# RWKV in a hybrid decoder step: the norm of the key as a scale of tokens in the chunk inverse instead of a factor of the features

## The chip, the core and the metric

The kernel runs on one core of one Trainium2 chip. The metric is the device time of one execution in microseconds (us), as the median of several runs. Time before the change: 991.74 us (three runs, 990.62 to 992.3).

## What is computed

One step of a layer in which two branches run beside each other on the same normalised input: a linear-attention branch (RWKV-7, 8 heads of 64 features) and a differential attention. Gates merge them, and a squared-ReLU MLP follows. There are 512 prompt tokens and 8 sequences of 8 tokens, 576 in all. The change lies in the RWKV branch. Cut to that:

```python
kk = hs((k * lp['k_k']).astype(f32))
kk = kk / jnp.maximum(jnp.linalg.norm(kk, axis=-1, keepdims=True), 1e-12)
k = k.astype(f32) * (1.0 + (a - 1.0) * lp['k_a'].astype(f32))
S, y = rwkv7_scan(S0, hs(r), hs(decay), hs(k), hs(v), -kk, kk * hs(a))
# scan, for each token:
sa = jnp.einsum('bhij,bhj->bhi', S, a_t)          # a_t = -kk
S = S * w_t + sa[..., None] * b_t + v_t[..., None] * k_t   # b_t = kk * a
y_t = jnp.einsum('bhij,bhj->bhi', S, r_t)
```

Each key is divided by its norm over the 64 features of its head. The normalised key enters the recurrence twice, as `-kk` and as `kk * a`, so that the square of the inverse norm stands in the product of the two.

## The kernel before, in words

Everything that is dense is streamed through TensorE (PE): a weight block of 128 columns comes in by DMA, ScalarE (ACT) makes a rounded half of it (`hi_...`), VectorE (DVE) the rest (`lo_...`), and three products for each slice of 128 features (high by high, high by low, low by high, lines 190 to 196, each over 288 tokens) accumulate in PSUM. In the trace and in the order these products are named after what they write: `ps_z` are the RWKV projections (function `shifted`, line 424), `ps_g` the gates (`gate`, line 444), `ps_brb` the attention branch's output projection (`branch_b`), and later `ps_bra`, `ps_wo`, `ps_dn` and the MLP's. All of them are issued by PE in a fixed order.

The RWKV branch works on four pairs of heads (`rwkv(hp)`, line 742), with tokens in chunks of 64: eight of the prompt and a ninth that holds the 64 sample tokens. For a pair the stages are:

1. Preparation. `sq` is the square of the scaled key (line 753), five small products `pn` sum it over the features of a head (line 756), `nr` is the sum with a floor, raised to -0.5 on GpSimd (POOL, line 760). POOL then spreads each token's factor over 64 columns (`nb`, line 763). Four transposes `pk` and one `pks` on PE (lines 791 to 793) turn that into feature layout in PSUM, and two DVE instructions (lines 794 and 796) multiply it with the key and `k_k` to `kk`, which overwrites `sq`. Meanwhile the products `pw` and `pa` (lines 769 and 772), ACT and DVE make the decays (`u`, `cum`, `pe`, `pinv`, `pm`), `aa`, `k2` and `rkp`; `pbn` (line 807) is a product of `rkp`. `KB` and `ST` (lines 814 to 821) are the scaled keys and receptances; `pA` (line 833) is their product for every chunk, which DVE masks into `ABR` and `ST`.
2. `pV`, `pK` are transposes, `pI` (line 865) the product with the sample tokens' states.
3. The inverse (lines 878 to 927): a unit triangular matrix of every chunk is inverted in blocks of 32 tokens by doubling. `DT` is a copy of the diagonal blocks, `Y` and its 32x32 transpose `X` the first level. Each of four levels has 32x32 products `pW`, an ACT copy `W`, products `pZ`, the DVE addition `X<-X,pZ` and the transpose `Y<-X`. `pWc` and `pC` then make the block off the diagonal, and ACT puts the parts together in `TT`. Between `pW`, `pZ`, `pWc` and `pC` the call `take(9)` (line 894) puts nine streamed products, so that PE has work while ACT and DVE answer.
4. `chain(pr)` (line 994): the eight chunks one after the other for two pairs together (`pch` in four roles; DVE and ACT between them).
5. The output of a pair (lines 946 to 983): group norm, transposes `pTy`, products `pg` with the output gate, and the vector `oa`.

How many streamed products stand between those stages is written by hand: `waiting` is a list of streams that have yet to run, and `take(n)` (line 216) issues the next n products of it at that place. Lines 1084 to 1104 hold the order of the stages and these numbers. A list scheduler then fixes the order of each engine's instructions, and `fill` keeps some products behind a given one. When the list is empty, `take` issues nothing; it is filled again behind the last inverse (line 1097).

Of the kernel before, what the change touches and what calls it, by code (L numbers as in the profile page):

```python
# [8 lines left out]
F32 = mybir.dt.float32  # L9
# [3 lines left out]
ALU = mybir.AluOpType  # L13
AX = mybir.AxisListType

P = 128
D = 1024
KT = D // P
NPR = 512
# [7 lines left out]
NCH = 9  # L27
# [5 lines left out]
V_MU, V_W0, V_A0, V_KK, V_KA, V_RK, V_LW, V_LB, V_GM, V_GF, V_GO, V_SUB, V_END = (  # L33
    0, 14, 18, 22, 26, 30, 34, 38, 42, 50, 58, 66, 67)
# [7 lines left out]
def tile_hybrid_step(ctx, tc, xT, xsT, ktab, vtab, s0T, ptab, w_in, vecs, w2a2, g2, lamv,  # L42
# [3 lines left out]
    PE, VE, AE, GE = nc.tensor, nc.vector, nc.scalar, nc.gpsimd  # L46
    PS = bass.MemoryType.PSUM

    def pool(name, bufs=1, stack=ctx, **kw):
        return stack.enter_context(tc.tile_pool(name=name, bufs=bufs, **kw))  # L50
# [6 lines left out]
    def act(out, in_, func=AF.Copy, **kw):  # L57
        ring["act"] = AE.activation(out=out, in_=in_, func=func, **kw)  # L58

    def tt(out, a, b, op, eng=None):  # L60
        ins = (eng or VE).tensor_tensor(out=out, in0=a, in1=b, op=op)  # L61
        if eng is None:
            ring["tt"] = ins

    def stt(out, a, s, b, op0, op1):
        VE.scalar_tensor_tensor(out=out, in0=a, scalar=s, in1=b, op0=op0, op1=op1)

    def ts(out, a, s1, op0, s2=None, op1=ALU.bypass, eng=None):
        (eng or VE).tensor_scalar(out=out, in0=a, scalar1=s1, scalar2=s2, op0=op0, op1=op1)

    def mm(out, lhsT, rhs, start=True, stop=True):
        ring["mm"] = PE.matmul(out=out, lhsT=lhsT, rhs=rhs, start=start, stop=stop)  # L72
        return ring["mm"]

    def tr(out, in_, idn):
        ring["mm"] = PE.transpose(out=out, in_=in_, identity=idn)
# [14 lines left out]
    MUL, ADD, SUB, MAX = ALU.mult, ALU.add, ALU.subtract, ALU.max  # L91
# [7 lines left out]
    stat = pool("stat", 2)  # L99

    def bank(name):
        return psw.tile([P, 512], F32, tag="w", name=name)

    def tbank(name):
        return psc.tile([P, 512], F32, tag="t", name=name)

    def cbank(i, name):
        return (psy if i else psc).tile([P, 512], F32, tag=f"c{i}", name=name)
# [3 lines left out]
    c = const.tile([P, C_END], F32, name="cst_sb")  # L112
    nc.scalar.dma_start(out=c, in_=cst)
    ident = c[:, C_ID:C_ID + P]
# [8 lines left out]
    mhalf = const.tile([P, 20], F32, name="mhalf")  # L123
# [10 lines left out]
    def v(i, n=1):  # L134
        return vec[:, i:i + n]
# [80 lines left out]
    def take(n):  # L216

        while waiting and n:
            if next(waiting[0], None) is None:
                waiting.pop(0)  # L220
            else:
                n -= 1
# [38 lines left out]
    rc = pool("rc", stack=ph1)  # L261
# [9 lines left out]
    with tc.tile_pool(name="xin", bufs=2, reuse_waits="tile") as xin:  # L271
# [6 lines left out]
        for k in range(0, KT, 4):  # L278
            for j in range(3):
                with prio(FEED + 1000 + 10 * k + j):  # L280
                    name = f"raw_{'qkv'[j]}0_{k}"
                    if k == 0:
                        raw = ring["pool"].tile([P, 4, P], F32, tag="raw", name=name, bufs=3)
                    else:
                        raw = zw.tile([P, 1 + NX], F32, tag="z" if j else "tz", name=name,
                                      bufs=2 if j else 1)[:, :4 * P].rearrange("p (k w) -> p k w", k=4)
# [12 lines left out]
        for k in range(KT):  # L299
            if k == 0:  # L300
                act(acc, xt[k], AF.Square)
            else:
                sq = xin.tile([P, NT], F32, name="sq")
# [10 lines left out]
    ts(mu1, v(V_MU, 14), -1.0, MUL, 1.0, ADD, GE)  # L314
    hw0 = rc.tile([P, 8], F32, name="hw0")
    ts(hw0, v(V_W0, 8), 0.5, MUL, 0.0, ADD, GE)
    ka2 = rc.tile([P, 8], F32, name="ka2")
    ts(ka2[:, 0:4], v(V_KA, 4), 0.5, MUL, 0.0, ADD, GE)
    ts(ka2[:, 4:8], v(V_KA, 4), -0.5, MUL, 1.0, ADD, GE)
# [345 lines left out]
    for h in range(HB):  # L665
        if h:
            qkv(h)
        for cc in range(2):
            GE.tensor_copy(
                out=qbd[64 * cc:64 * cc + 64, :, h, 8 * cc:8 * cc + 8],  # L670
                in_=qT[64 * cc:64 * cc + 64, h, NPR:].rearrange("p (b q) -> p b q", b=NB))
# [45 lines left out]
    rt = pool("rt", 2, stack=rk, reuse_waits="tile")  # L717

    def ch(a):
        return a.rearrange("p (c t) -> p c t", t=64)  # L720

    def m3(ap_, n):
        q, w = ap_.shape
        return ap_.rearrange("p (o w) -> p o w", o=1).broadcast_to([q, n, w])
# [15 lines left out]
    halves = [(par, slice(64 * par, 64 * par + 64)) for par in range(2)]  # L740

    def rwkv(hp):
        e = hp % 2
        own = pair.setdefault(hp // 2, {})
        hs = slice(hp * P, (hp + 1) * P)
        r, k, vv = Pt[hp], Pt[4 + hp], Pt[8 + hp]

        def tmp(tag, bufs=1):
            return rt.tile([P, NT], F32, tag="T", name=f"{tag}_{hp}", bufs=6)


        sq = tmp("sq")
        act(sq, k, AF.Square, scale=v(V_KK + hp))
        pn = bank(f"pn{hp}")
        for t, o in enumerate(toks):
            mm(pn[:, 2 * t:2 * t + 2], sq[:, o:o + P], c[:, C_HS:C_HS + 2])
        (fill if hp != 2 else take)(8)
        nr = stat.tile([P, 10], F32, tag="nr", name=f"nr{hp}")
        ts(nr, pn[:, 0:10], 1e-24, MAX)
        GE.tensor_tensor(out=nr, in0=nr, in1=mhalf[:, :10], op=ALU.pow)  # L760

        nb = rt.tile([P, 5, P], F32, tag="G", name=f"nb{hp}", bufs=3)
        own["nb"] = GE.tensor_copy(out=nb.rearrange("p t (a d) -> p (t a) d", a=2),
                       in_=nr.rearrange("p (a o) -> p a o", o=1).broadcast_to([P, 10, 64]))
        u = tmp("u")
        aa = tmp("aa")
        for t0, n in HALF:
# [15 lines left out]
        pinv = tmp("pinv")  # L783
        act(pinv, cum, AF.Exp, scale=KAPPA)
        tt(cum, cum, u, SUB)
        pm = u
        act(pm, cum, AF.Exp, scale=-KAPPA)

        kk = sq
        pk, pks = bank(f"pk{hp}"), bank(f"pks{hp}")  # L790
        for t in range(4):
            tr(pk[:, t * P:(t + 1) * P], nb[:, t], ident)
        tr(pks[:, :P], nb[:, 4], ident)
        stt(kk[:, :NPR], k[:, :NPR], v(V_KK + hp), pk, MUL, MUL)
        pk = pks
        stt(kk[:, NPR:], k[:, NPR:], v(V_KK + hp), pk[:, 64:P], MUL, MUL)


        k2 = tmp("k2")
        act(k2, aa, AF.Identity, scale=ka2[:, hp:hp + 1], bias=ka2[:, 4 + hp:5 + hp])  # L800
        tt(k2, k2, k, MUL)
# [7 lines left out]


        KB = rt.tile([P, NCH, 2, 64], F32, tag="KB", name=f"KB{hp}", bufs=1)
        stt(aa, aa, 1.0, kk, ADD, MUL)
        ST = []
        for par, rows in halves:
            stt(KB[rows, :, par], ch(aa)[rows], 0.5, ch(pinv)[rows], MUL, MUL)
            tt(KB[rows, :, 1 - par], ch(k2)[rows], ch(pinv)[rows], MUL)
            st = rb_.tile([P, NCH, 2, 64], F32, tag=f"ST{par}", name=f"ST{par}_{hp}")
            with tc.issue_after(own["nb"].ins) if hp == 0 else nullcontext():
                GE.memset(st[64 - 64 * par:128 - 64 * par], 0.0)
            stt(st[rows, :, 0], ch(kk)[rows], -1.0, ch(pm)[rows], MUL, MUL)  # L820
            tt(st[rows, :, 1], ch(r)[rows], ch(pe)[rows], MUL)
            ST.append(st)
        KBc = [KB[:, ci].rearrange("p a t -> p (a t)") for ci in range(NCH)]
# [3 lines left out]
        for par in range(2):  # L827
            rows = slice(64 * par, 64 * par + 64)
# [38 lines left out]
        for par in range(2):  # L867
            rows = slice(64 * par, 64 * par + 64)
# [9 lines left out]
        DT = rt.tile([P, NCH, 32], F32, tag="DT", name=f"DT{hp}")  # L878
        for g in range(4):
            gs = slice(32 * g, 32 * g + 32)  # L880
            act(DT[gs], ABR[gs, :, 0, 32 * (g % 2):32 * (g % 2) + 32])
        Y = rt.tile([P, NCH, 32], F32, tag="Y", name=f"Y{hp}", bufs=2)
        X = rt.tile([P, NCH, 32], F32, tag="X", name=f"X{hp}", bufs=2)
        tt(Y, DT, m3(c[:, C_LM:C_LM + 32], NCH), MUL)
        tt(Y, Y, m3(c[:, C_I32:C_I32 + 32], NCH), ADD)
        VE.transpose(out=X, in_=Y)

        def blocks(ps, lhs, rhs, n):
            for ci in range(n):
                for g in range(4):  # L890
                    gs = slice(32 * g, 32 * g + 32)
                    last = mm(ps[gs, ci * 32:ci * 32 + 32], lhs[gs, ci], rhs[gs, ci])
            with tc.issue_after(last.ins):
                take(9)
            return ps[:, :n * 32].rearrange("p (c s) -> p c s", c=n)
# [3 lines left out]
        for l in range(1, 5):  # L899

            n = NCH if l < 3 else 8
            DM = rt.tile([P, NCH, 32], F32, tag="DM", name=f"DM{hp}_{l}")
            tt(DM[:, :n], DT[:, :n], m3(c[:, C_LM + 32 * l:C_LM + 32 * l + 32], n), MUL)
            W = rt.tile([P, NCH, 32], F32, tag="W", name=f"W{hp}_{l}")
            act(W[:, :n], blocks(tbank(f"pW{hp}{l}"), DM, X, n))
            tt(X[:, :n], X[:, :n], blocks(tbank(f"pZ{hp}{l}"), Y, W, n), ADD)
            VE.transpose(out=Y[:, :n], in_=X[:, :n])
        TT = rb_.tile([P, NCH, 64], F32, tag="TT", name=f"TT{hp}")
        pW = tbank(f"pWc{hp}")
# [8 lines left out]
        for ci in range(8):  # L918
            for b0, b1 in quads:
                mm(pC[b0, ci * 32:ci * 32 + 32], W[b1, ci], Y[b1, ci])  # L920
        for b0, b1 in quads:
# [149 lines left out]


    gens = [rwkv(hp) for hp in range(4)]

    def run(*stages):
        for hp in stages:
            while Pt[8 + hp] is None:
                take(2)
            next(gens[hp], None)
# [2 lines left out]
    ga = [gate(g) for g in range(KT)]  # L1082
    waiting += ga[:5]
    run(0, 0)
    take(221)
    run(0, 1, 1)
    take(106)
    run(1)
    chain(0)
    run(0, 1, 2)  # L1090
# [1 line left out]
    run(2, 3)  # L1092
    take(85)
    run(2, 0, 1, 3)
    take(38)
    run(3)
    waiting += [x for d in range(KT) for x in [branch_b(d)] + ga[5:][d:d + 1]]
    run(0, 1)
# [55 lines left out]
    for i, d in enumerate((0, 4, 1, 5, 2, 6, 3, 7)):  # L1154
# [4 lines left out]
        k = d % 4  # L1159
# [26 lines left out]
        for j, (t0, n) in enumerate(HALF):  # L1186
            o = acc[:, t0:t0 + n]
            if i == 0:
                act(o, ya[:, d, t0:t0 + n], AF.Square)
            else:  # L1190
                sq = cbank(j, f"sq{d}{j}")[:, :n]
# [133 lines left out]
    rows = []  # L1325
    for d, n in enumerate((None, "t1", "b11", "t2", "b21", "t3", "b22", "t4")):
        if n:
            t = fp.tile([P, 2, 4, 288], F32R, tag=f"h_{n}", name=f"w3_{d}", bufs=1)
            t = t.rearrange("p i k t -> p (i k t)")
# [196 lines left out]
```

## Time and profile before

One execution was profiled. Its own time was 993.35 us, its span from the first to the last instruction 991.6 us, so that 1.75 us lie around the span; it is 1.61 us above the median of the three runs.

| | before |
|---|---|
| median of three runs | 991.74 us |
| profiled execution, its time | 993.35 us |
| its span | 991.6 us |
| PE, time with a matmul in work | 964.5 us (97%) |
| DVE busy | 694.3 us (70%) |
| ACT busy | 495.1 us (50%) |
| POOL busy | 91.0 us (9%) |
| mean granted TensorE clock | 0.989 |

The page of the profile gives the busy time of each engine, the chain of work that ended last, and groups of instructions with their mean duration and the idle time ahead of them. The list of waits says for what PE waited in total. The timeline gives the start of each instruction, its duration and, in brackets, how long the engine had been idle and who released it. A matmul's end is modelled, so the distance from one start to the next is the better measure of what it costs. A product in fp32 shows as two records; a transpose and the streamed products as one. The view by stretches gives the clock that TensorE was granted (PEclk, 1.00 is full speed) and how many instructions began in a stretch.

The RWKV part of the program lies between 174 us (first `pn`) and 510 us.

### The profile page before, as it was taken

To read this page: it belongs to the slowest core of one execution; us is meant where nothing else is said; L and a number is where in the kernel's file an instruction comes from. 1 tells how busy PE (TensorE), PEld (TensorE's weight loads), DVE (VectorE), ACT (ScalarE), POOL (GpSimd) and SP (SyncE) were. 2 spreads that over 40 slices of the span, in tenths; PEclk is the share of its full clock that TensorE was granted. 3 is DMA by queue.
4 is the path that set the end of the run, shared out by engine and by line. 5 is a ranking of instruction groups with operands and counts; after the bars stand their busy time and mean duration, and the time that the engine had idled before them with its cause. 6 is when DMAs were issued, how large, how long until landed. Compare 5 with 4: busy or idle time off the path is not lost.

```text
span 991.6 us, 24377 instructions
## 1 busy us (share of the span) xinstructions
PE 964.5 (97%) x9996; PEld 913.4 (92%) x9996; DVE 694.3 (70%) x1459; ACT 495.1 (50%) x1084; POOL 91.0 (9%) x171
## 2 busy tenths in 40 slices
PE   8999999999999998999999999999999999999996
PEld 8999989898986898988889999999999999999996
DVE  6698566874945779445688898966666666666744
ACT  6576455354344455443344767444444444444732
POOL 2611100401003230001200000000000000000001
PEclk9999999999999999999999999999999999999998
DMA  7322673221112215222377642222222222221402
GB/s 266 128 76 76 210 220 117 80 59 52 44 63 74 79 62 161 79 70 100 121 234 223 209 132 97 87 94 86 86 86 86 85 86 86 86 87 42 136 3 95
DMA packets 50832, 105.73 MB, mean 107 GB/s; under 512 B 6066, under 2 KB 8114, under 8 KB 50594
## 3 DMA queue, kind: packets, MB, share of 16 engines
q1 hardware_dynamic: 47442, 96.95, 30.4%
q0 software_dynamic: 1648, 5.35, 1.5%
q8 instruction: 78, 1.28, 0.6%
q10 hardware_dynamic: 1632, 1.89, 0.5%
q14 instruction: 32, 0.26, 0.1%
HBM read 89.38 MB, written 14.78 MB: 105 GB/s over the span
## 4 chain that ended last, share of the span: by engine, by line
PE 83%; DVE 6%; issue 6%; ACT 3%; POOL 1%; DMA 0%; SPq 0%; DVEq 0%; POOLq 0%; ACTq 0%
PE ps_dn L72 21%; PE ps_z L72 8%; PE ps_g L72 7%; PE ux L1250 5%; PE ua L1250 5%; PE ps_wo L72 4%; PE ps_brb L72 3%; PE ps_k L72 3%; PE ub L1250 3%; PE ud L1250 3%; PE ps_bra L72 3%; PE uc L1250 3%; PE pch L1010 2%; PE ps_q L72 2%; PE ps_v L72 2%
## 5 line engine op out<-in xcount | busy, mean ns | idle before, releaser
L72 PE MATMUL ps_dn<-q,hi_dn 128*128 128x288 f32 x768 | 154.7, 296 | 0.0
L72 PEld LDWEIGHTS ps_dn<-q,hi_dn 128*128 128x128 f32 x768 | 122.9, 188 | 1.4
L72 PE MATMUL ps_dn<-q,lo_dn 128*128 128x288 f32 x384 | 113.3, 295 | 0.0
L72 PE MATMUL ps_g<-xl,hi_g 128*128 128x288 f32 x256 | 79.7, 311 | 0.0
L72 PE MATMUL ps_g<-xh,lo_g 128*128 128x288 f32 x256 | 79.2, 309 | 0.0
L72 PE MATMUL ps_g<-xh,hi_g 128*128 128x288 f32 x256 | 78.5, 307 | 0.0
L72 PEld LDWEIGHTS ps_dn<-q,lo_dn 128*128 128x128 f32 x384 | 72.2, 188 | 0.0
L72 PE MATMUL ps_z<-xh,lo_z 128*128 128x288 f32 (+1 forms) x224 | 69.2, 310 | 0.0
L72 PE MATMUL ps_z<-xh,hi_z 128*128 128x288 f32 (+1 forms) x224 | 68.0, 303 | 0.0
L72 PE MATMUL ps_z<-xl,hi_z 128*128 128x288 f32 (+1 forms) x224 | 66.9, 299 | 0.0
L61 DVE TENSOR_TENSOR ya<-ya,ps_dn 128x288 f32<-128x288 f32 x96 | 43.3, 451 | 27.6 <-PE ps_dn L72 27.5
L58 ACT ACTIVATE hi_dn<-raw_dn 128x512 fp32r<-128x512 f32 x48 | 30.1, 628 | 56.2 <-PE ps_dn L72 56.1
L58 ACT ACTIVATE c<-c 128x288 f32<-128x288 f32 x112 | 48.8, 440 | 9.4 <-DVE c L61 7.7
L1250 PE MATMUL ux<-h_t,hi 128*128 128x288 f32 x256 | 52.4, 297 | 0.0
L1250 PE MATMUL ua<-h_b,hi 128*128 128x288 f32 x256 | 52.2, 296 | 0.0
L72 PEld LDWEIGHTS ps_g<-xl,hi_g 128*128 128x128 f32 x256 | 48.9, 191 | 1.5
L72 PEld LDWEIGHTS ps_g<-xh,lo_g 128*128 128x128 f32 x256 | 49.0, 191 | 1.3
L72 PEld LDWEIGHTS ps_g<-xh,hi_g 128*128 128x128 f32 x256 | 48.8, 191 | 1.0
L58 ACT ACTIVATE hi<-a 128x1024 fp32r<-128x1024 f32 (+1 forms) x32 | 27.1, 846 | 43.1 <-PE ps_dn L72 34.9
L61 DVE TENSOR_TENSOR lo<-s,hi 128x1024 fp32r<-128x1024 f32 x32 | 39.2, 1224 | 10.4 <-ACT hi L58 10.3
L72 PE MATMUL ps_dn<-q,w 128*128 128x320 f32 (+1 forms) x336 | 46.3, 298 | 0.0
L72 PEld LDWEIGHTS ps_dn<-q,w 128*128 128x128 f32 x336 | 45.3, 190 | 0.1
(391 smaller groups left out, 2789.1 us busy)
## 6 DMA issues: line engine op xcount, KB each, us to landing
a<-in_w_up_dram SPq DMA_DIRECT2D x32, 512.0 KB, 3.3
raw_dn<-in_w_down_dram SPq DMA_DIRECT2D x64, 256.0 KB, 2.8
raw_g<-in_w_in_dram SPq DMA_DIRECT2D x32, 256.0 KB, 3.0
raw_z<-in_w_in_dram SPq DMA_DIRECT2D x28, 256.0 KB, 3.1
gt_d<-gg SPq DMA_DIRECT2D x16, 288.0 KB, 2.3
g<-gt_d SPq DMA_DIRECT2D x16, 288.0 KB, 3.6
kp<-in_ktab_dram SPq DMA_DIRECT2D x16, 256.0 KB, 4.0
vp<-in_vtab_dram SPq DMA_DIRECT2D x16, 256.0 KB, 3.4
```

Source lines behind the costliest of these rows:

```text
L58: ring["act"] = AE.activation(out=out, in_=in_, func=func, **kw)
L61: ins = (eng or VE).tensor_tensor(out=out, in0=a, in1=b, op=op)
L72: ring["mm"] = PE.matmul(out=out, lhsT=lhsT, rhs=rhs, start=start, stop=stop)
L1010: ring["mm"] = PE.matmul(out=ps[rows, e], lhsT=lhs, rhs=rhs, start=first and e == 1, stop=True, skip_group_check=True)
L1250: ring["mm"] = PE.matmul(out=ps[:, :288], lhsT=l[:, k], rhs=hb[blk][:, h, k], start=start and i == 0, stop=i == 11, skip_group_check=skip)
```

## The change

The norm no longer touches the features. `nr` becomes the reciprocal of the squared norm, by a DVE instruction instead of the power on POOL. Six small POOL copies put it in a table `dn` with one column for each chunk and one row for each token of the two heads. `KB` and `ST` are built from the key without its norm (with `k_k` and its half or its negative as a scalar per feature), and the missing factor is put in as a scale of rows: `DT` is multiplied by `dn` ahead of the first level of the inverse, and `X` once more after the last level. The POOL copy `nb`, the transposes `pk` and `pks` and the two DVE instructions for `kk` go. Three of the hand-written counts are changed: 221 to 161 ahead of the first pair's inverse, 106 to 226 ahead of the second's, 38 to 18 ahead of the fourth's.

```diff
         ts(nr, pn[:, 0:10], 1e-24, MAX)
-        GE.tensor_tensor(out=nr, in0=nr, in1=mhalf[:, :10], op=ALU.pow)
-
-        nb = rt.tile([P, 5, P], F32, tag="G", name=f"nb{hp}", bufs=3)
-        own["nb"] = GE.tensor_copy(out=nb.rearrange("p t (a d) -> p (t a) d", a=2),
-                       in_=nr.rearrange("p (a o) -> p a o", o=1).broadcast_to([P, 10, 64]))
+        VE.reciprocal(out=nr, in_=nr)
+        dn = stat.tile([P, NCH], F32, tag="dn", name=f"dn{hp}", bufs=4)
+        n2 = nr.rearrange("p (t a) -> p t a", a=2)
+        for par, rows in halves:
+            GE.tensor_copy(out=dn[rows, 0:8:2], in_=n2[0:64, 0:4, par])
+            GE.tensor_copy(out=dn[rows, 1:8:2], in_=n2[64:128, 0:4, par])
+            own["nb"] = GE.tensor_copy(out=dn[rows, 8:9], in_=n2[64:128, 4:5, par])
...
-        kk = sq
-        pk, pks = bank(f"pk{hp}"), bank(f"pks{hp}")
-        for t in range(4):
-            tr(pk[:, t * P:(t + 1) * P], nb[:, t], ident)
-        tr(pks[:, :P], nb[:, 4], ident)
-        stt(kk[:, :NPR], k[:, :NPR], v(V_KK + hp), pk, MUL, MUL)
-        pk = pks
-        stt(kk[:, NPR:], k[:, NPR:], v(V_KK + hp), pk[:, 64:P], MUL, MUL)
...
-        stt(aa, aa, 1.0, kk, ADD, MUL)
+        stt(aa, aa, 1.0, k, ADD, MUL)
...
-            stt(KB[rows, :, par], ch(aa)[rows], 0.5, ch(pinv)[rows], MUL, MUL)
+            stt(KB[rows, :, par], ch(aa)[rows], hkk[rows, hp:hp + 1], ch(pinv)[rows], MUL, MUL)
...
-            stt(st[rows, :, 0], ch(kk)[rows], -1.0, ch(pm)[rows], MUL, MUL)
+            stt(st[rows, :, 0], ch(k)[rows], nkk[rows, hp:hp + 1], ch(pm)[rows], MUL, MUL)
...
             act(DT[gs], ABR[gs, :, 0, 32 * (g % 2):32 * (g % 2) + 32])
+        byd = dn.rearrange("p (c o) -> p c o", o=1).broadcast_to([P, NCH, 32])
+        tt(DT, DT, byd, MUL)
...
             tt(X[:, :n], X[:, :n], blocks(tbank(f"pZ{hp}{l}"), Y, W, n), ADD)
+            if l == 4:
+                n = NCH
+                tt(X, X, byd, MUL)
             VE.transpose(out=Y[:, :n], in_=X[:, :n])
...
-    take(221)
+    take(161)
     run(0, 1, 1)
-    take(106)
+    take(226)
...
-    take(38)
+    take(18)
     run(3)
```

What this does to the order of the instructions is shown at two places, in rows of the order that was built from each kernel. A number behind a name tells tiles of the same name apart.

First, PE at the second pair, from the end of `pI` to the first products of the inverse, `pW`. Before:

```order
L72 MATMUL pI_3915<-ST_1_3829,s_1_3905 64x16
L72 MATMUL pI_3915<-ST_1_3835,s_1_3905 64x16
L72 MATMUL pW_4109<-X_4101,DM_1_4106 32x32 x36
L72 MATMUL ps_g_1_4065<-xl,hi_g_0_4056 128x288
L72 MATMUL ps_g_1_4065<-xh,lo_g_0_4057 128x288
```

After, PE at the same place, the end of `pI`:

```order
L72 MATMUL pI_3829<-ST_1_3720,s_1_3796 64x16
L72 MATMUL pI_3829<-ST_1_3726,s_1_3796 64x16
L72 MATMUL ps_z_0_3991<-xh,hi_z_0_3983 128x288
L72 MATMUL ps_z_0_3991<-xl,hi_z_0_3983 128x288
L72 MATMUL ps_z_0_3991<-xh,lo_z_0_3984 128x288
```

Before, `pW` stands directly behind `pI`. After, 136 streamed products (48 of `ps_z`, 88 of `ps_g`) stand between them. At the first pair it is the other way: 119 products between `pI` and `pW` before, 58 after.

Second, PE in the inverse of the fourth pair, before, from the last of the nine products behind the last `pZ` on (`pTy` and `pg` belong to the outputs of the first two pairs):

```order
L72 MATMUL ps_g_1_6398<-xh,hi_g_1_6393 128x288
L72 MATMUL ps_g_1_6398<-xl,hi_g_1_6393 128x288
L72 MATMUL pWc_6633<-X_6229,ABR_5456 32x32 x16
L76 MATMUL pTy_0_6682<-cst_sb,y_4568 128x128 x4
L76 MATMUL pTy_448_6691<-cst_sb,y_4568 128x128
L72 MATMUL pg_6697<-P_2066,wg 128x288
L72 MATMUL pC_6653<-Y_6228,Wc_6634 32x32 x16
```

After, PE in the same inverse, from the third level's `pW` on:

```order
L72 MATMUL pW_6490<-X_6284,DM_3_6487 32x32 x32
L76 MATMUL pTy_0_6682<-cst_sb,y_4648 128x128 x4
L72 MATMUL pZ_6524<-W_3_6489,Y_6283 32x32 x32
L76 MATMUL pTy_448_6691<-cst_sb,y_4648 128x128
L72 MATMUL pg_6697<-P_2070,wg 128x288
L72 MATMUL pW_6562<-X_6284,DM_4_6559 32x32 x32
L72 MATMUL pg_6700<-P_2070,wg 128x288
L72 MATMUL pZ_6596<-W_4_6561,Y_6283 32x32 x32
L76 MATMUL pTy_0_6706<-cst_sb,y_4648 128x128 x4
L76 MATMUL pTy_448_6715<-cst_sb,y_4648 128x128
L72 MATMUL pg_6721<-P_2070,wg 128x288
L72 MATMUL pWc_6633<-X_6284,ABR_5528 32x32 x16
```

Before, nine streamed products stand in each gap of this inverse up to `pWc`. After, the list is empty from the third level's `pW` on, and what stands in the gaps is the outputs' `pTy` and `pg`. DVE at the same place, after, from the third level's addition to the end of the inverse:

```order
L61 TENSOR_TENSOR X_6284<-X_6284,pZ_6524 128x256
L69 TENSOR_SCALAR oa_6681<-oa_6681,vec 128x576
L908 STREAM_TRANSPOSE Y_6283<-X_6284 128x256
L61 TENSOR_TENSOR oa_6681<-oa_6681,bv_2803 128x576
L61 TENSOR_TENSOR oa_6681<-oa_6681,pg_6697 128x288
L61 TENSOR_TENSOR oa_6681<-oa_6681,pg_6700 128x288
L61 TENSOR_TENSOR X_6284<-X_6284,pZ_6596 128x256
L61 TENSOR_TENSOR X_6284<-X_6284,dn_5461 128x288
L908 STREAM_TRANSPOSE Y_6283<-X_6284 128x288
```

The instructions for `oa` stood behind the inverse on DVE before; four of them now stand within it.

More of the change, by code (lines that the diff above doesn't have):

```diff
@@ L316, in tile_hybrid_step @@
     ts(hw0, v(V_W0, 8), 0.5, MUL, 0.0, ADD, GE)
+    nkk = rc.tile([P, 4], F32, name="nkk")
+    ts(nkk, v(V_KK, 4), -1.0, MUL, 0.0, ADD, GE)
+    hkk = rc.tile([P, 4], F32, name="hkk")
+    ts(hkk, v(V_KK, 4), 0.5, MUL, 0.0, ADD, GE)
     ka2 = rc.tile([P, 8], F32, name="ka2")
```

## The prediction

> **What bounds the kernel now.** I read the page first. It says that PE is the engine to follow: a matmul is in work in 97% of the span, and 83% of the chain that ended last is PE's.
>
> ```profile
> span 991.6 us, 24377 instructions
> PE 964.5 (97%) x9996; PEld 913.4 (92%) x9996; DVE 694.3 (70%) x1459; ACT 495.1 (50%) x1084; POOL 91.0 (9%) x171
> PE 83%; DVE 6%; issue 6%; ACT 3%; POOL 1%; DMA 0%; SPq 0%; DVEq 0%; POOLq 0%; ACTq 0%
> ```
>
> So the time can fall in three ways only: fewer matmuls, shorter waits of PE (991.6 - 964.5 = 27 us in the whole span), or a clock that falters less. The list of what PE waited for names the removed `nb` at its head, and `rkp`, which the change moves:
>
> ```profile
> PE pk L76 <- POOL nb L763: 2.0, 2, 1.4
> PE pbn L72 <- DVE rkp L66: 1.5, 2, 1.1
> ```
>
> Then the timeline of PE around the waits in the RWKV part (start, duration, in brackets the idle time and its releaser), first at the first pair:
>
> ```profile
> 181.27 0.66 PE L76 MATMUL pk<-cst_sb,nb 128*128 128x128 f32 x4 [1.44 <-POOL nb L763]
> 181.79 0.38 PE L72 MATMUL ps_z<-xh,hi_z 128*128 128x296 f32 x1
> 182.01 0.30 PE L72 MATMUL ps_z<-xl,hi_z 128*128 128x296 f32 x1
> 182.14 0.30 PE L72 MATMUL ps_z<-xh,lo_z 128*128 128x296 f32 x1
> ```
>
> and at the later pairs (275.80 is the second pair, 315.81 the third, the others the fourth):
>
> ```profile
> 275.80 0.39 PE L72 MATMUL pW<-X,DM 32*32 32x32 f32 x24 [0.26 <-DVE X L886]
> 315.81 0.33 PE L76 MATMUL pk<-cst_sb,nb 128*128 128x128 f32 x1 [0.60 <-POOL nb L763]
> 380.04 0.51 PE L72 MATMUL pbn<-rkp,cst_sb 128*128 128x288 f32 x1 [1.11 <-DVE rkp L66]
> 392.29 0.63 PE L76 MATMUL pV<-cst_sb,P 128*128 128x128 f32 x4 [0.32 <-DVE ST L61]
> 393.77 0.34 PE L1010 MATMUL pch<-SVU,ST 128*64 128x64 f32 x4 [0.85 <-ACT SVU L58]
> ```
>
> Last, the stretches. Streamed products alone (`ps_z`, `ps_g`), with the count in brackets (one begins every 0.13 us at 182.01, so that 3.4 us hold 26):
>
> ```profile
> 239.80:243.20 3.40, 1.26 (x8) 1.00 0.30 81
> 273.90:277.30 3.40, 0.75 (x5) 1.00 0.02 5
> 359.30:362.70 3.40, 1.29 (x10) 1.00 0.02 5
> ```
>
> and all of PE, with the granted clock behind the count, for two of these and for the stretch behind each of the three:
>
> ```profile
> 239.80:243.20 3.40, 3.40 (x82) 1.00 0.30 81
> 359.30:362.70 3.40, 3.40 (x52) 1.00 0.02 5
> 243.20:246.60 3.40, 3.40 (x21) 0.50 0.04 13
> 277.30:280.70 3.40, 3.40 (x83) 0.51 0.06 11
> 362.70:366.10 3.40, 3.40 (x12) 0.50 0.23 78
> ```
>
> Where 8, 5 and 10 streamed products stood among 32x32 products and products of a few columns, the clock was halved for the next 3.4 us. A halved stretch that PE could have filled costs up to 1.7 us, so these three hold about 5 us.
>
> **The change part by part.** The sum is made against the profiled execution (993.35 us, span 991.6 us), and the difference is put on the median, 991.74 us. The DVE, ACT and tail durations come from these groups:
>
> ```profile
> L61 DVE TENSOR_TENSOR DM<-DT,cst_sb 128x288 f32<-128x288 f32 x8 | 3.6, 450 | 1.5 <-PE pW L72 1.5
> L61 DVE TENSOR_TENSOR X<-X,pZ 128x256 f32<-128x256 f32 x8 | 3.4, 420 | 7.7 <-PE pZ L72 7.7
> L907 DVE STREAM_TRANSPOSE Y<-X 128x256 f32<-128x256 f32 x8 | 3.6, 445 | 0.3
> L66 DVE SCALAR_TENSOR_TENSOR sq<-P,vec,pk 128x512 f32<-128x512 f32 x4 | 2.9, 731 | 0.9 <-PE pk L76 0.9
> L66 DVE SCALAR_TENSOR_TENSOR KB<-aa,pinv 64x576 f32<-64x576 f32 x8 | 6.0, 749 | 0.1
> L69 DVE TENSOR_SCALAR oa<-oa,vec 128x576 f32<-128x576 f32 x2 | 1.2, 580 | 1.1 <-ACT oa L58 1.1
> L61 DVE TENSOR_TENSOR oa<-oa,bv 128x576 f32<-128x576 f32 x2 | 1.5, 758 | 0.1
> L58 ACT ACTIVATE oa<-pTy 64x256 f32<-64x256 f32 x8 | 3.0, 378 | 0.7 <-PE pTy L76 0.6
> L58 ACT ACTIVATE Wc<-pWc 32x256 f32<-32x256 f32 x8 | 3.0, 376 | 0.5 <-PE pWc L72 0.2
> L58 ACT ACTIVATE TT<-Y 32x288 f32<-32x288 f32 x16 | 7.0, 438 | 3.4 <-DVE Y L907 3.2
> ```
>
> (1) The transposes. `pk` and `pks` hold PE from 181.27 to 181.79, 0.52 us, and the step back to streaming takes 0.22 instead of 0.13: 0.61 us for a pair, four pairs: **-2.4 us**. This is PE's own time and nothing hides it.
>
> (2) The waits for `nb`, 1.44 and 0.60 us, go. What is late next: at the first pair `pbn` needs `rkp`. It now has 49 products ahead of it behind `pa` instead of 82, so PE comes there 33 x 0.13 + 1.44 + 0.61 = 6.3 us earlier. On DVE `rkp` passes three `KB`, an `ST` and `aa` (0.75 each), a `Z` and a `lo_z` (about 0.45 and 0.69), and `sq` (0.73) goes: 5.6 us earlier. That gives back 0.7, and at the third pair `pch` behind `pk` waits for its own chain; I take 0.7 there too: **-0.6 us**, between -2.0 and +0.5.
>
> (3) `pbn` at the second and fourth pair waited 1.5 us together. There PE comes 37 and 20 products earlier (5.4 and 3.2 us with the transposes), `rkp` passes four `KB` or three `ST` and more and comes at least 4 us earlier. About half of the wait should go: **-0.8 us**, between -1.5 and 0.
>
> (4) Second pair: `pW` no longer stands behind `pI`, 136 products do. The wait of 0.26 us goes: **-0.3 us**. The thin stretch that halved the clock at 277.3 now ends with `pI`. By the order it still holds `pV`, `pch`, `pK` and `pI` with their waits, which together can still fill 3.4 us, so a halved stretch may remain; I put half of one: **-0.8 us**, between +1.7 and -3.4.
>
> [...]
>
> (5) Fourth pair: the chain's first `pch` stood between `pV` and `pK` and waited 0.85 us for `SVU`; it moves behind `pWc`, and nine products now stand ahead of `pV` (0.32). **-1.0 us**, between -1.2 and 0.
>
> (6) Fourth pair's inverse: the nine products in each gap are used up from the third level's `pW` on. Before:
>
> ```profile
> 428.60 0.75 PE L72 MATMUL pW<-X,DM 32*32 32x32 f32 x64
> 429.46 0.38 ACT L58 ACTIVATE W<-pW 128x256 f32<-128x256 f32 x1 [3.47 <-PE pW L72]
> 441.07 0.33 PE L1010 MATMUL pch<-R,TT 64*64 64x64 f32 x4 [0.18 <-issue]
> ```
>
> From `pW` to the chain's `pch` that uses `TT`: 12.5 us. A bare half level takes 0.75 + 0.11 + 0.38 and about 0.07 = 1.31 us. After, counted from `pW`: `pZ` at 1.3, next `pW` at 2.6, `W` done at 3.9. DVE has an `oa` instruction between the addition and `Y`, which waits for six ACT copies of `pTy` (to 3.2): `Y` done at 3.2 + 0.58 + 0.45 = 4.3, `pZ` at 4.4. Three more `oa` instructions end at 4.3 + 0.76 + 2 x 0.45 = 5.9, the addition at 6.4, the multiplication by `dn` at 6.8, `pWc` at 6.9; two `Wc`, `pC`, six copies into `TT` (0.42 each): `pch` at 11.0, 1.5 us earlier. But 42 streamed products less lie in it (50 before, 8 after, 5.5 us), against five more `pTy`, three more `pg` and six more `pch` that would have cost 2.3 elsewhere. PE loses 5.5 - 2.3 - 1.5 = **+1.7 us**, between 0 and +7.
>
> (7) No cost: the reciprocal, six POOL copies (`dn` is used 20 us later; `nb` and the power had more time on POOL), and `DT` by `dn`. `X` by `dn` (0.45 us) is covered for pairs one to three:
>
> ```profile
> 237.83 0.75 PE L72 MATMUL pZ<-W,Y 32*32 32x32 f32 x64
> 239.93 0.25 PE L72 MATMUL pWc<-X,ABR 32*32 32x32 f32 x4
> ```
>
> 2.10 us lie between them, and 0.75 + 0.42 + 0.45 with three steps of 0.07 need 1.83. Uncovered it would cost 0.45 for each pair.
>
> Sum: -2.4 - 0.6 - 0.8 - 0.3 - 0.8 - 1.0 + 1.7 = **-4.2 us, 987.5 us**.
>
> **The rivals.** *The first inverse loses its cover (no change).* Before, `X` was ready 10.6 us ahead of `pW`:
>
> ```profile
> 211.38 0.47 DVE L886 STREAM_TRANSPOSE X<-Y 128x288 f32<-128x288 f32 x1
> 222.44 0.35 PE L72 MATMUL pW<-X,DM 32*32 32x32 f32 x18
> ```
>
> 61 products fewer take 7.9 us of that, and `DT` by `dn`, a `DM` and a `lo_z`, which now stand ahead of `X` on DVE, 1.6: 1.1 us are left. Each further delay on DVE or ACT (the evacuations and `tz` ahead of `X`) counts in full. If `X` is 4 us later than I think, PE waits 3 and the time is 990.5 us. For it speaks that so little is left; against it, that the evacuations come with PE's products, which are also earlier.
>
> *The bare tail is far longer (slower).* The outputs' work on ACT (eight copies of 0.38, four of 0.22, 3.9 us) and on DVE (2 x (0.58 + 0.76 + 2 x 0.45), 4.5 us) stands within the fourth inverse. I counted 1.2 us of these 8.4. If all of it lies on the inverse's path, the time is 987.5 + 7.2 = 994.7 us. It decides from 6.2 us of the 7.2. Against it: most of these copies have a level's time to run beside `pZ` and `X`.
>
> *The halved stretches stay as they are (988.3 us)*: what thins out at one place may thin out at another, and PE's thin stretches at the first and third pair (239.8, 359.3) are not changed.
>
> *All goes well:* the second pair's halved stretch goes for certain and (2) and (3) reach their lower ends: -4.2 - 0.9 - 1.4 - 0.7 = -7.2, 984.5 us.
>
> **How the numbers follow.** Forecast 0.50, halved stretches unchanged 0.09, all well 0.07, first inverse bare 0.24, tail bare 0.10. A difference of 0.2%, 2.0 us, is about what a measurement of this kernel can tell from none, so faster means below 989.7: 0.50 + 0.09 + 0.07 = 0.66; same 0.24; slower 0.10. The range goes from the case in which all is well, 984.5, to 991.2, which takes in the bare first inverse (990.5) with 0.7 to spare and leaves out the bare tail.
>
> **What would show it.** Right: no wait at 181; DVE about as busy as before, PE with 20 matmuls fewer; no wait of `pW` at the second pair; `pZ` and `pWc` of the fourth inverse waiting 2 to 3 us in all for `W`, `Y` and `X`; at most three halved stretches. Wrong: `pW` of the first pair waiting more than 1 us for `X`; waits of over 5 us in the fourth inverse; a halved stretch in it; waits of `pA` for `KB`.

## The result and the profile after

Over twelve runs of each kernel the median was 991.61 us before and 989.05 us after, ratio 0.9975 with a 95% interval of 0.9963 to 0.9986: **2.5 us faster**. Run again beside before on another chip (e5 below), the changed kernel gave 0.9979 (0.9969 to 0.9989). Ratios and mean clocks here and below leave out three executions that took far longer than the rest: 1146.0 us of e1, 1821.6 us of e3 and 3169.8 us of before. The prediction was 987.5 us, 4.2 us below the median then shown, with 984.5 to 991.2 as its range: the direction is right, the gain was put 1.7 us too high.

The profiled execution took 988.29 us. Its page has these lines:

```profile
span 986.2 us, 24366 instructions
PE 958.3 (97%) x9976; PEld 908.0 (92%) x9976; DVE 694.7 (70%) x1463; ACT 494.9 (50%) x1084; POOL 81.4 (8%) x189
```

PE has 20 matmuls fewer and DVE is as busy as before, as the prediction's signs had it. PE's busy time fell by 6.2 us (964.5 to 958.3), but the time in which it was not in work did not: 27.1 us of the span before, 27.9 after. So the gain in these two profiles lies in fewer products and in the clock, and not in waits that became shorter as a whole. The span is 5.4 us shorter than that of before, twice what the medians differ by. Part of the reason is the clock: the profile of before has three halved stretches in the RWKV part and a mean clock of 0.989, that of after none there and 0.996. In 86 further runs of before the mean clock averaged 0.9946 and was never under 0.991; in 24 runs of after it averaged 0.9958. So the profile of before that the prediction worked from shows a rare execution, and the change gives back on average 0.0012 of the clock, at most 0.0012 x 990 = 1.2 us, not three stretches.

Rows of the RWKV part in the list of what PE waited for, after:

```profile
PE pZ L72 <- issue: 4.0, 6, 1.0
PE pch L1011 <- DVE SVU L69: 1.5, 2, 1.0
PE pbn L72 <- DVE rkp L66: 1.4, 2, 1.0
PE pch L1011 <- ACT SVU L58: 1.2, 2, 1.0
PE pW L72 <- issue: 0.6, 1, 0.6
PE pK L76 <- ACT SVU L58: 0.4, 1, 0.4
PE pA L72 <- DVE KB L61: 0.3, 1, 0.3
```

`nb` is gone from it, as foreseen. `pbn` still waits, and `pch` waits more than before. At the head stands something the prediction had not priced, `pZ <- issue`. In the profile of before these rows were

```profile
PE pZ L72 <- issue: 1.8, 3, 1.0
PE pch L1010 <- ACT SVU L58: 1.5, 3, 0.9
PE pch L1010 <- DVE SVU L69: 0.5, 1, 0.5
```

"issue" is a wait for nothing that the trace shows. The timeline gives the places the prediction named (start, duration, in brackets the idle time): `pbn` of the first pair, `pW` of the first pair, `pch` at the second, `pW` at the second, `pch` just ahead of the third, `pK` at the fourth.

```profile
185.78 0.99 PE L72 MATMUL pbn<-rkp,cst_sb 128*128 128x288 f32 x3 [0.98 <-DVE rkp L66]
212.95 0.44 PE L72 MATMUL pW<-X,DM 32*32 32x32 f32 x30
258.96 0.34 PE L1011 MATMUL pch<-SVU,ST 128*64 128x64 f32 x4 [1.00 <-ACT SVU L58]
280.62 0.57 PE L72 MATMUL pW<-X,DM 32*32 32x32 f32 x44
313.43 0.62 PE L1011 MATMUL pch<-SVU,ST 128*64 128x64 f32 x13 [0.98 <-DVE SVU L69]
394.28 0.41 PE L76 MATMUL pK<-cst_sb,KB 128*128 128x128 f32 x2 [0.23 <-DVE ST L61]
```

Neither `pW` waited: the first inverse kept its cover. By how little, DVE's timeline says:

```profile
211.91 0.47 DVE L884 STREAM_TRANSPOSE X<-Y 128x288 f32<-128x288 f32 x1
```

`X` was ready at 212.38, 0.57 us ahead of `pW`, where the prediction had counted 1.1 us.

Last the fourth inverse, from the third level's `pW` on, in PE's timeline:

```profile
425.36 0.75 PE L72 MATMUL pW<-X,DM 32*32 32x32 f32 x64
426.72 0.45 PE L72 MATMUL pZ<-W,Y 32*32 32x32 f32 x31
428.15 0.46 PE L72 MATMUL pZ<-W,Y 32*32 32x32 f32 x33 [0.98 <-issue]
429.28 0.75 PE L72 MATMUL pW<-X,DM 32*32 32x32 f32 x64
430.65 0.43 PE L72 MATMUL pZ<-W,Y 32*32 32x32 f32 x26
432.00 0.54 PE L72 MATMUL pZ<-W,Y 32*32 32x32 f32 x38 [0.92 <-issue]
433.65 0.54 PE L72 MATMUL pWc<-X,ABR 32*32 32x32 f32 x22
...
438.19 0.45 PE L1011 MATMUL pch<-R,TT 64*64 64x64 f32 x8 [0.43 <-issue]
```

Both `pZ` groups break within their 64 products, for nearly 1 us each, and nothing in the trace releases them. The waits in the bare inverse (bare: without streamed products in its gaps) are these, and not the waits for `W`, `Y` and `X` that the prediction listed as its sign. The chain's `pch` that uses `TT` came 12.8 us after `pW`, not 11.0.

### The profile page after: what moved, and what is told of

Same layout as the page of the kernel before. It is cut to its first block, busy times and chain, and to the rows that moved or that the text cites. A ratio compares the mean times of both kernels' runs of the same rounds, so it can differ in the third digit from the quotient of the medians.

```text
span 986.2 us, 24366 instructions
## 1 busy us (share of the span) xinstructions
PE 958.3 (97%) x9976; PEld 908.0 (92%) x9976; DVE 694.7 (70%) x1463; ACT 494.9 (50%) x1084; POOL 81.4 (8%) x189
## 4 chain that ended last, share of the span: by engine, by line
PE 85%; DVE 6%; ACT 4%; issue 2%; DMA 1%; POOL 0%; SPq 0%; DVEq 0%; ACTq 0%; POOLq 0%
PE ps_dn L72 20%; PE ps_g L72 9%; PE ps_z L72 8%; PE ua L1251 5%; PE ux L1251 5%; PE ps_wo L72 4%; PE pch L1011 3%; PE ps_brb L72 3%; PE ps_k L72 3%; PE uc L1251 3%; PE ub L1251 3%; PE ud L1251 2%; PE ps_bra L72 2%; PE ps_q L72 2%; PE ps_v L72 2%
## 5 line engine op out<-in xcount | busy, mean ns | idle before, releaser
L72 PE MATMUL ps_z<-xh,hi_z 128*128 128x296 f32 (+1 forms) x224 | 67.3, 300 | 0.0
L58 ACT ACTIVATE hi<-a 128x1024 fp32r<-128x1024 f32 (+1 forms) x32 | 27.1, 846 | 43.3 <-PE ps_dn L72 34.9
```

## The experiments

All ratios are to the kernel before in runs on the same chip; four chips served. One 0.001 is 1 us. Mean clock is the average over a kernel's runs; that of before was 0.9952 beside e1 to e4, 0.9942 beside e5 to e8, 0.9941 beside e9 to e11 and 0.9944 beside e12.

| kernel | counts | ratio, 95% interval | mean clock |
|---|---|---|---|
| e5, the changed kernel again | 161, 226, 18 | 0.9979 (0.9969 to 0.9989) | 0.9955 |
| e1, new arithmetic, old counts | 221, 106, 38 | 1.0018 (1.0003 to 1.0033) | 0.9911 |
| e2, old arithmetic, new counts | 161, 226, 18 | 1.0031 (1.0016 to 1.0046) | 0.9930 |
| e10, old arithmetic, two counts | 161, 166, 38 | 0.9980 (0.9970 to 0.9989) | 0.9952 |
| e6, new arithmetic, two counts | 161, 166, 38 | 0.9957 (0.9943 to 0.9971) | 0.9945 |
| e3, new arithmetic | 161, 184, 18 | 0.9995 (0.9984 to 1.0005) | 0.9948 |
| e7, e5 with 11 products a gap | 161, 172, 18 | 0.9951 (0.9932 to 0.9970) | 0.9940 |
| e9, new arithmetic, 10 a gap | 161, 148, 38 | 0.9930 (0.9914 to 0.9945) | 0.9954 |
| e4, e5 with twenty idle transposes | 161, 226, 18 | 1.0051 (1.0033 to 1.0069) | 0.9901 |
| e12, e6 with twenty idle transposes | 161, 166, 38 | 1.0018 (1.0002 to 1.0034) | 0.9933 |
| e8, e5 without `dn` | 161, 226, 18 | 1.0004 (0.9989 to 1.0019) | 0.9940 |
| e11, e5, warm-up longer | 161, 226, 18 | 1.0054 (1.0035 to 1.0073) | 0.9928 |

**Either half alone.** e1 is the changed kernel with the old counts:

```diff
-    take(161)
+    take(221)
     run(0, 1, 1)
-    take(226)
+    take(106)
...
-    take(18)
+    take(38)
```

> The new arithmetic with the three old counts (221, 106, 38). Theory A (the prediction's terms: the gain is the transposes and the waits around them, the counts are worth -0.4 us in all): -2.4 - 0.6 - 0.8 = -3.8 us against before, ratio 0.9962, and the fourth inverse keeps its nine products in each gap, so that waits of pZ marked issue stay near the 1.8 us of before. Theory B (the gain is the clock, which the counts brought: three halved stretches in the RWKV part of the profile of before, none in that of after): the pW of the second pair stands directly behind pI and pch again, halved stretches come back (two or three in the profile), and the ratio is 0.999 or above.

e2 is the kernel before with the new counts, the same lines the other way.

> The old arithmetic (nb, transposes, kk) with the three new counts (161, 226, 18). Theory A: the counts alone are worth -0.3 - 0.8 - 1.0 + 1.7 = -0.4 us, ratio 0.9996, same within the measurement. Theory B: no halved stretch in the second pair, at most one in all, and most of the gain of the whole change: ratio 0.9975 to 0.9985. Theory C (the bare fourth inverse costs more than term 6 says, because PE's own instructions come too slowly there): ratio above 1.000, with 3 us or more of pZ waits marked issue.

Both were slower than before: e1 by 1.8, e2 by 3.1 us, though together they make a kernel that is 2.5 us faster. Theory A misses e1 by 5.6 us; B holds there, with three halved stretches in the RWKV part (at 263.5, 277.2 and 362.5 us). For e2 A and B both fall. Only C has the ratio above 1, but it asked for 3 us of issue waits at `pZ`, and the profile has 1.2 at `pZ` and 1.8 at `pW`, of which 0.9 us lie in the fourth inverse. So C is not confirmed by e2, and what made e2 slow stays open. e1's profile shows waits and a clock that take up the transposes' gain. PE's list of waits and timeline:

```profile
PE pbn L72 <- DVE rkp L66: 2.3, 3, 1.0
PE ps_g L72 <- DVE Z L61: 2.0, 1, 2.0
PE pW L72 <- DVE X L884: 1.4, 1, 1.4
```

```profile
263.38 0.46 PE L72 MATMUL ps_g<-xh,hi_g 128*128 128x288 f32 x1 [1.99 <-DVE Z L61]
276.83 0.36 PE L72 MATMUL pW<-X,DM 32*32 32x32 f32 x20 [1.45 <-DVE X L884]
```

and the granted clock behind these thin places, in the view by stretches:

```profile
263.50:266.90 3.40, 3.40 (x16) 0.50 0.29 77
277.20:280.60 3.40, 3.40 (x87) 0.50 0.02 5
```

With 106 products, the second pair's `pW` stands right behind `pI`, and the wait for `X`, 0.26 us before, is now 1.45: `DT` by `dn` lies on this path, and PE comes earlier by the transposes that are gone. e1's mean clock of 0.9911 is 0.0041 below that of before on the same chip (0.9952): up to 4 us.

**Two counts of three.** e6 keeps 161 but has 166 and 38, so that the fourth inverse keeps nine products in each gap (it is covered); e10 is the same with the old arithmetic; e5 is the changed kernel, as a control beside e6.

```diff
     take(161)
     run(0, 1, 1)
-    take(226)
+    take(166)
...
-    take(18)
+    take(38)
```

> The changed kernel with 161, 166 and 38: sixty products move from the first pair to the second as before and none is taken from the fourth inverse, which keeps nine in each gap; 76 instead of 136 stand between pI and pW at the second pair. If the bare fourth inverse costs what term 6 says (+1.7), this is 0.9975 - 0.0017 = 0.9958. If it costs nothing, because its gaps are filled with the outputs' own products and the streamed ones run at full rate elsewhere, it is 0.9975. If taking products from the second pair costs more than that (as the run with 184 and 18 at 0.9995 hints), it is 0.999 or above, with new waits between pI and pWc of the second pair or in the chain behind it.

> The kernel before with 161 and 166 for 221 and 106, 38 as it was: sixty streamed products moved from ahead of the first inverse to ahead of the second, with the old arithmetic. With the new arithmetic the same move measured 0.9957 against 1.0018, -6.1 us. If the gain is the products' alone (a second pair in which pW no longer stands behind pI, one halved stretch less): 0.994 to 0.997 here too. If it needs the new arithmetic (the old one has no multiplication of DT ahead of the second pair's pW, waited there for 0.26 us only, and needs the sixty products at nb and rkp no less): 0.999 to 1.002.

> The changed kernel unaltered, beside before on the same chip as the next three, since the first four runs spread more than those of the comparison. If the comparison holds here: ratio 0.9975 (0.996 to 0.999) and at most one halved stretch in the RWKV part of its profile. If its profile without any halved stretch was luck: one to three of them, and a ratio nearer 1.

These three and before make a chain of steps. Moving sixty products from the first pair to the second: -2.0 us with the old arithmetic (e10, between its two expectations), so that the gain is in part the products' own. The new arithmetic at those counts: 0.9957 - 0.9980, -2.3 us (two chips, each against before). Taking another sixty to the second pair, and so leaving the fourth inverse bare: 0.9979 - 0.9957, +2.2 us on one chip, with intervals that overlap by 0.0002. The three add up to e5's own -2.1 by their making, so the sum is no test of them. e5 itself came out as expected, with one halved stretch in the RWKV part. In e6 the fourth inverse has no break (a wait for issue within a group of 32x32 products); its timeline of PE, third and fourth level:

```profile
421.56 0.75 PE L72 MATMUL pW<-X,DM 32*32 32x32 f32 x64
423.63 0.75 PE L72 MATMUL pZ<-W,Y 32*32 32x32 f32 x64
426.61 0.75 PE L72 MATMUL pW<-X,DM 32*32 32x32 f32 x64
428.68 0.75 PE L72 MATMUL pZ<-W,Y 32*32 32x32 f32 x64
```

e3 covers the fourth inverse in another way, with 184 for 226 and 18 kept.

> The changed kernel with 226 lowered to 184, so that the list still holds products in the fourth inverse (nine in each gap up to pWc) and 94 instead of 136 stand between pI and pW at the second pair. If term 6 is right, the bare inverse's loss of +1.7 us goes: -4.2 us against before, ratio 0.9958. If instructions that come too slowly make it dearer (three waits of 0.94 to 1.17 us marked issue inside it in the profile of after), about 3 us go: ratio 0.9945. If PE is full whatever the order, the 42 products cost the same elsewhere: ratio 0.9975 as in the changed kernel.

It came out at 0.9995, 2 us worse than the changed kernel, which no theory had. Its fourth inverse is covered, and yet the longest break of all the profiles stands in it, within a `pZ`:

```profile
428.48 0.25 PE L72 MATMUL pZ<-W,Y 32*32 32x32 f32 x3 [1.85 <-issue]
```

In all, `pZ` waits 4.3 us for issue in e3, no less than in the changed kernel (4.0), and `pZ` and `pW` together 0.8 us in e6 against 4.4 in e5. So cover alone does not take these waits away, and how much of e6's 2.2 us is the cover and how much the place at which PE's instructions broke off was not separated. The scheduler's order in e3 differs elsewhere too. DVE's timeline, and PE's behind it:

```profile
370.25 0.76 DVE L61 TENSOR_TENSOR y<-y,var 128x576 f32<-128x576 f32 x1 [1.91 <-POOL var L243]
...
371.75 0.68 DVE L61 TENSOR_TENSOR lo_g<-raw_g,hi_g 128x512 fp32r<-128x512 f32 x1
```

```profile
372.48 0.40 PE L72 MATMUL ps_g<-xh,lo_g 128*128 128x288 f32 x1 [2.03 <-DVE lo_g L61]
```

An output's `y<-y,var` waits 1.91 us for a power on POOL, and behind it in DVE's queue stands the low half `lo_g` that the streamed products need. DVE waits so three times (5.2 to 5.7 us in all) in e2, e3, e4 and e8, once (1.6) in the changed kernel, e5 and e11, and twice (3.4 to 3.7) in before, e1, e6, e7, e10 and e12; e9 has it three times too (4.5) and is fast. In e3 PE's wait of 2.03 us is in the trace; how the 2 us by which e3 is slower divide between this and the breaks was not isolated.

**PE's own instructions.** In all fourteen profiles there are 60 breaks of over 0.3 us, from the start of one product to the start of the next, within groups of 32x32 products. If all of PE's instructions in the trace are counted through, its weight loads and matmuls and also its semaphore and drain instructions, all 60 breaks end 193 or 194 beyond a multiple of 256. The page's row for the instruction queue (packets, MB, share of time) fits a block of that size:

```profile
q8 instruction: 78, 1.28, 0.5%
```

These are 78 packets of 16.4 KB. PE has 2 x 9976 weight loads and matmuls, 255.8 for a packet; for which engine the packets are, the row does not say. Each break ends 1.15 to 1.60 us after the last such packet. e7 makes a block last longer with two more products in each gap:

```diff
             with tc.issue_after(last.ins):
-                take(9)
+                take(11)
...
-    take(226)
+    take(172)
```

> The changed kernel with eleven instead of nine products in each gap of the inverses and 226 lowered to 172, so that the fourth inverse is as bare as before. Theory C (PE's own instructions come too slowly for the 32x32 products: all waits marked issue in six profiles stand at the same place, 193 or 194, in a count of PE's instructions by 256): with two more products a gap the same 256 instructions take longer, the waits of the first three inverses (0.49, 0.37, 1.03 and 0.76 in the profile of after) fall under 1 us in all, and the time falls by 1.5 to 2 us: 0.9955 to 0.996. If those waits are made up elsewhere or PE is full anyway: 0.9975.

e11 moves the blocks against the program:

```diff
         for _ in range(9):
             mm(up[:, :P], onesP, onesP)
+    with prio(FEED - 1):
+        for _ in range(24):
+            mm(up[:, :1], onesP, ones1)
```

> The changed kernel with 24 products of one column added to the warm-up at the start (they show as 48 records, 96 instructions of PE). If the waits marked issue come from the way PE's instructions are brought in, 256 at a time, they move with the count: still 193 or 194 beyond a multiple of 256, that is 48 records earlier in the program, at other places of the inverses, about as many and as long. If they come from the pZ products themselves (banks, weights), they stay at the records where they were (in the changed kernel the 51st of the second pZ and the 32nd and 27th of the third and fourth of the fourth inverse). The time: 0.9975 plus or minus 0.002.

e7 is 2.8 us faster than e5 on the same chip (0.9951 against 0.9979, intervals that overlap by 0.0001), and its first two inverses have no break: the 2.65 us of the changed kernel there are gone. A new break of 1.10 us stands in the third inverse, which has none in the changed kernel, so the waits fell less than expected. Here are the last two `pZ` of its second pair on PE:

```profile
285.95 0.75 PE L72 MATMUL pZ<-W,Y 32*32 32x32 f32 x64
290.62 0.75 PE L72 MATMUL pZ<-W,Y 32*32 32x32 f32 x64
```

A rival stands: e7 has 57 products and e6 has 76 between `pI` and `pW` of the second pair, where the changed kernel has 136, and no run kept the 136 and changed the gaps or the cover alone. That fewer products at this place are part of both gains is not ruled out. Against it speak e3, which has 94 there and was slower, and e11 (next), which kept the 136 and gained as its breaks fell from 5.9 us in all to 3.4.

In e11 the breaks are still at 193 or 194, and so at other products, mostly in `pW` (list of waits):

```profile
PE pW L72 <- issue: 1.8, 4, 0.9
PE pZ L72 <- issue: 0.6, 1, 0.6
```

That they belong to blocks of 256 and not to certain products is shown. There are five of them and not seven, and from the first `pn` to the end e11's profile is 2.1 us shorter than that of after; that was luck of the place. The time, 1.0054, missed what was expected, since the added products took 9.1 us at the start (last section).

**The transposes.** e4 puts twenty transposes without use into the changed kernel, e12 into e6:

```diff
+        pk, pks = bank(f"pk{hp}"), bank(f"pks{hp}")
+        for t in range(4):
+            tr(pk[:, t * P:(t + 1) * P], ident, ident)
+        tr(pks[:, :P], ident, ident)
         k2 = tmp("k2")
```

> The changed kernel with twenty transposes put back as work without use (four into pk and one into pks for a pair, of a constant, so that they wait for nothing). Term 1 says 0.61 us a pair: +2.4 us against the changed kernel, ratio to before 0.9975 + 0.0024 = 1.000. If the transposes were hidden behind waits that are still there (pbn waits 1.0 us for rkp at the first pair and 0.4 at the second), 1.0 to 1.4 us of them cost nothing: ratio 0.9985 to 0.999.

> The changed kernel with 161, 166, 38 (measured 0.9957) and the twenty transposes put back as work without use, of a constant, so that they wait for nothing; with these counts the order of the other products changes in few places. Term 1 (-2.4 us for the twenty, nothing hides them): 0.9957 + 0.0024 = 0.998, the ratio of the old arithmetic with the same counts (0.9980). If the waits of pbn for rkp (2.2 us in the profile without them) take up the transposes: 0.9957 to 0.9965. Above 0.9995 some other wait of 2 us or more has come up, as in the first run with transposes, and the run prices nothing.

Both cost far more than 2.4 us: 7.2 and 6.1 (each ratio against before on its own chip). Both orders changed at the third and fourth pair, where e4 waits 2.4 us for `gg` and e12's `pbn` waits 2.5 us, so the times price nothing, as e12's expectation allowed. What can be read is the stretch from the first pair's `pn` to the third's in the profiles of e6 and e12, where both issue the same work but for two sets of transposes and neither has a halved stretch. The two starts in PE's timeline, of e6 and of e12:

```profile
173.94 1.28 PE L72 MATMUL pn<-cst_sb,sq 128*128 128x2 f32 x10
306.51 1.28 PE L72 MATMUL pn<-cst_sb,sq 128*128 128x2 f32 x10
```

```profile
173.82 1.28 PE L72 MATMUL pn<-cst_sb,sq 128*128 128x2 f32 x10
307.77 1.28 PE L72 MATMUL pn<-cst_sb,sq 128*128 128x2 f32 x10
```

132.57 us against 133.95: 0.69 us for a set, where term 1 said 0.61. That the two agree is in part luck. Over the same stretch PE's waits differ by 0.7 us (4.4 in e6, 5.1 in e12), 0.35 of it at `pZ` for issue, and by pairs the difference is 0.29 us (second `pn` at 231.47 and 231.65) and 1.08.

**The multiplications by `dn`.** e8 leaves out both, and so the norm (the key's scalar `nkk` becomes a small constant times `k_k`):

```diff
-        tt(DT, DT, byd, MUL)
...
-                tt(X, X, byd, MUL)
```

> The changed kernel without the two multiplications by dn (the norm is left out, and a constant in the key's scalar keeps the values small). Term 7 says they are covered at pairs one to three and that X by dn costs 0.45 us at the fourth: 0.997. If they stood on the path at every pair (0.45 us for DT by dn and 0.45 for X by dn, eight times): -3.6 us against the changed kernel, 0.994.

With eight DVE instructions less it was 2.5 us slower than e5: again another order, with a wait of 2.3 us of `ps_g` for `gg`. It settles nothing on term 7.

**Both cures.** e9 has the counts 161, 148, 38 and `take(10)`.

> The changed kernel with 161, 148, 38 and ten products in each gap: the two edits that measured 0.9957 and 0.9951 together, as far as the list of streamed products reaches (34 between pI and pW at the second pair, nine to ten in the fourth inverse up to its last level). If the fourth inverse's cover and the waits for PE's own instructions are two separate losses: below 0.995 and under 1.5 us of pZ waits marked issue. If they are the same loss seen twice, or if the second pair misses the products: 0.9955 to 0.9975.

0.9930, **6.9 us faster than before** and 4.5 faster than the change (five runs). Its list of waits has of the 4.0 us only

```profile
PE pZ L72 <- issue: 0.7, 2, 0.4
```

By the expectation the two losses were separate. It is one kernel with five runs, and its interval (0.9914 to 0.9945) overlaps that of e7.

## Why the prediction was right in sign and too high

*Step 1, not contradicted, but not isolated.* -2.4 forecast. Two sets of transposes lengthen the stretch by 1.38 us between e6 and e12, with 0.7 us more of waits in it. The new arithmetic at fixed counts is worth -2.3, but that holds the waits for `nb` and the rest of the change too.

*Steps 2, 3 and 5, right in kind, too large.* They gave -2.4 us together. The waits for `nb` went, `pbn` at the first pair took 0.98 back (0.7 expected), `pV` and `pch` at the fourth pair stopped waiting but for 0.23 at `pK`. But the wait of `pch` for `SVU` at the second pair grew from 0.42 to 1.00 us, which no step had, and just ahead of the third pair `pch` waited 0.98. By the lists, `nb`, `pbn`, `pch`, `pV` and `pK` have 6.0 us before (2.0, 1.5, 1.5 + 0.5, 0.3, 0.2) and 4.7 after (1.4, 1.5 + 1.2, 0.4 + 0.2): -1.3.

*Step 4, right in size.* The wait of `pW` is gone. Half a halved stretch, 0.8 us, was taken; the mean clocks give 1.2 us at most. The prediction worked from one profile with three such stretches, which is not usual, and only the half stretch in the sum kept this from mattering. The time in which PE was in work did not tell the clock here: in the profile of before it was halved behind 3.40 us with PE in work for 3.40 (from 239.8 and 359.3), and its mean was 0.989 there and 0.996 in that of after, with PE in work for 97% of both spans. The kernels' mean clocks lie between 0.9901 and 0.9961.

*Step 6, right in kind, too small.* +1.7 forecast; covering the inverse again in e6 gave 2.2 against e5, which also has sixty products more at the second pair, and e3 gave the reverse, so this size is not isolated. Two slips met in the term. The 50 products counted before included the nine ahead of `pW`; 41 (37 of `ps_g`, 4 of `ps_brb`) lie between 428.60 and 441.07, so 33 and not 42 went. And the bare levels do not run at the pace of ACT and DVE alone: the two breaks in them hold 1.9 us of PE's waits, and the stretch took 12.8 us, not 11.0. With both put right the term is 33 x 0.13 - 2.3 + (12.8 - 12.5) = 2.3, an estimate from these rows.

*Step 7, as far as the trace shows right:* no `pWc` stands in the list of waits, and the first `pW` did not wait. Of the signs against the prediction one came, and small: `pA` for `KB`, 0.3 us.

With these sizes: -2.4 - 1.3 - 0.3 - 0.8 + 2.2 = -2.6, and 2.5 was measured. So close a sum is in part luck: -2.4 and -0.8 are the forecast's own, the others come from one or two profiles, and the breaks in the first two inverses, 2.65 us after against 1.2 before, stand in no term. The rivals: the first inverse kept its cover, with 0.57 us to spare, so that this rival was closer than the sum said; the bare tail was no 7 us.

What the prediction did not see is that the parts depend on each other through the order. The new arithmetic without the new counts, or all three of these without it, is slower than before. One change of order is in every profile but those of before and e10: 102 streamed products stand between `pI` and `pW` of the third pair, with the fourth pair's first products among them, where before and e10 have 8. What it costs or gains was not measured. In e1 the waits and the clock are seen that take up the gain; for e2, e3, e4, e8 and e12 it stays open how much is DVE's order, how much the clock and how much PE's breaks.

## What to carry to other kernels

Where streamed products are dealt out by hand as cover, a change of the arithmetic and a new deal belong together: the same arithmetic was worth +1.8 us with the old counts and -2.3 with two new ones, and the counts alone -2.0 or +3.1, by which of them were changed. Price a stretch of small products with its breaks too (0.37 to 2.05 us each in these profiles), and look in the trace for where it breaks off: cover helped in e6, and e3's covered inverse still had a break of 1.85 us. And take the clock from the mean over many runs; one profile had twice the loss that is usual.

## What was not expected of the hardware

- The breaks within groups of 32x32 products stand at the same place in a count of PE's instructions by 256 (193 or 194): 60 of 60, 0.37 to 2.05 us from one product to the next. The bare inverse of the fourth pair went through 256 instructions in 4.11 and 3.85 us (breaks ending at 424.04, 428.15, 432.00).
- The clock was halved in one execution of a program and not in another. Around the second pair's `pn`, the changed kernel run again (0.50) and the changed kernel (1.00) have:

```profile
233.20:236.60 3.40, 3.40 (x18) 0.50 0.08 21
```

```profile
231.40:234.80 3.40, 3.40 (x51) 1.00 0.02 5
234.80:238.20 3.40, 3.22 (x19) 1.00 0.24 77
```

- A lower mean clock went with a longer time, and by how much differed by kernel: of e2's twelve runs, three with a mean clock of 0.987 to 0.989 took 998.4 to 999.5 us, three with 0.996 took 992.1 to 993.4, some 0.8 us for 0.001. A straight line through the runs of before gives only 0.3 to 0.4 us for 0.001, on each of the four chips.
- Products of one column at the start of the program are not free: e11's 24, each with its own 128x128 fp32 weights, show as

```profile
5.12 10.24 PE L72 MATMUL warmup<-ones,onesP 128*128 128x1 f32 x48
15.22 0.59 PE L72 MATMUL ps_q<-xh,hi_q 128*128 128x288 f32 x1
```

0.21 us a record, and the first streamed product came at 15.22 us instead of 6.14. Without these 9.1 us e11's median is 988.0. Part of the price is the pace at the start: the streamed products behind them (16.33, 16.57, 16.81 us) begin every 0.24 us up to about 20 us, against 0.13 later, although the view by stretches gives a clock of 1.00 there. The ten records of `pn`, of two columns and with 128x128 weights as well, begin every 0.11 us.
